# The norm between two layers: g and b applied on ScalarE where the output is transposed, and to the residual later

## The chip, the cores and the metric

The kernel runs on one core of a Trainium2 chip. The metric is the device time in microseconds (us) of one execution. A core has five engines that work side by side, each through its own list of instructions: TensorE (PE, matrix products; PEld is its loading of weights), VectorE (DVE), ScalarE (ACT), GpSimd (POOL) and SyncE (SP, which here only issues DMAs). Engines wait for one another through semaphores.

## The reference: what is computed

Two post-norm layers over 256 tokens of width 2048, in f32. A layer projects x, runs three groups of heads (chunked attention, gated linear attention, and cross-attention into 256 memory tokens), gates their outputs, projects back and normalizes:

```
h = x @ w_in                               # 6672 columns, split into the groups' inputs
mkv = mem @ w_mem_kv                       # memory keys and values
y = concat(y_a * silu(a_z), y_b * silu(b_z), y_m * silu(m_z))
out = y @ w_out
x = layer_norm(alpha * x + out, ln_g, ln_b)

layer_norm(x, g, b) = (x - mean(x)) * rsqrt(var(x) + 1e-5) * g + b      # over the 2048 columns
```

g and b are vectors over the 2048 columns, one pair for each layer. This case is about the norm that ends the first layer: its result is both the operand of the second layer's projections and the residual that the second layer adds at its own end.

## The kernel before, in words

*Weights and parts.* Every f32 weight is split into a high part and the low part that remains, and each product is made of three: high by high, low by high, high by low. A weight piece (`piece`, L129) is loaded by SP into `raw`, cast to its high part `wh` by ScalarE (L117) and subtracted to its low part `wl` by VectorE (L118); the pool `wp` holds four pieces of each kind. `parts` (L115) does the same for operands. These loads and splits are given a high priority (`AHEAD`).

*Two forms of projection.* In `ws_group` (L253) the weights are stationary and the result comes out transposed, in two halves of four pieces each; a piece is 16 matmuls. In `as_group` (L271) the tokens are stationary and the result has tokens on the partitions; it takes eight pieces (twelve matmuls each). Both call `tick()` after each piece.

*What sets the order.* PE and SP run their instructions as the program writes them (`manual_schedule`, L50). The order on VectorE, ScalarE and GpSimd is set at build time by a planner that weighs priorities against its own estimates of durations. The small work of the heads, and the transposition between layers, is written as generators: `tick()` (L53) takes the next due step of at most two active ones, and a step's `yield n` puts the next one n pieces later. `finish` (L70) runs ticks until the given generators are done, so steps that are left come back to back.

*The end of a layer.* The output projection runs over four column blocks of 512 (loop at L821, `as_group` at L862). After each block VectorE adds the residual (`add_residual`, L571) and takes statistics (L573). The residual `res` is one tile of 128 partitions, two token halves t, and 2048 columns. Rows of g and b for each block, spread over all 128 partitions, are loaded on POOL's queue into scratch buffers (L822 to L824); the eight of them are all of the pool `sc`.

*The norm between the layers* (`norm_between`, L575): the mean and variance (L581), `rstd` by `rsqrt` (L284: a square root on ScalarE, then four small VectorE instructions), and `nmr` = -mean * rstd (L583). Then eight chunks of res, a column block n by a token half t. Five are done by VectorE in two instructions each (L592, L593); three (`LN_POOL`, L30) by one ScalarE activation (L588) and a multiply and an add on GpSimd (L589, L590).

*The start of the second layer* (L734 to L743): the memory values G_MV by `as_group`, while the norm runs, then the memory keys G_MK by `ws_group`. Beside G_MK the generator `transposed` (L544) turns res into the operand of the projections: eight pairs of column blocks of 128, each with four PE transposes into a PSUM bank (L555), a cast to the high part by ScalarE and a subtract by VectorE (L556). It yields 2, so four pairs fit between the eight pieces of G_MK and the last four follow at once in `finish` (L743). The next projection, G_BQK (L748), uses this operand, a quarter (two pairs) to each piece; then come two value groups (L772, L773) and the gated linear attention (`gla`, L304), whose tiles `pairs0` and `pairs1` and whose output `yraw` (tags yr0 to yr3) matter below.

The last layer's norm (`norm_last`, L610) is a function of its own and is not touched.

Of the kernel before, what the change touches and what calls it, by code (L numbers as in the profile page):

```python
# [8 lines left out]
F32 = mybir.dt.float32  # L9
# [3 lines left out]
AF = mybir.ActivationFunctionType  # L13
ALU = mybir.AluOpType
# [4 lines left out]
P = 128  # L19
D = 2048  # L20
T = 256
# [5 lines left out]
RMS_EPS = 1e-6  # L27
LEVELS = (32, 16, 8, 4, 2, 1)
WO_N = 4
LN_POOL = ((1, 1), (2, 1), (3, 1))  # L30


G_MK, G_MV, G_BQK, G_AQ0, G_AK0, G_AQ1, G_AK1, G_MQ, G_BZ, G_AZ0, G_AZ1, G_MZ, G_WO = range(13)
# [4 lines left out]
def hybrid_trunk_kernel(  # L38
# [7 lines left out]
    pe, dve, act, pool, sp = nc.tensor, nc.vector, nc.scalar, nc.gpsimd, nc.sync  # L46
# [4 lines left out]
    waiting, active, done, now = [], [], set(), [0]  # L51

    def tick():  # L53

        now[0] += 1
        while True:
            while waiting and len(active) < 2:
                active.append((waiting.pop(0), 0))
            due = [e for e in active if e[1] <= now[0]]
            if not due:  # L60
                return
            active.remove(due[0])
            g = due[0][0]
            after = next(g, None)
            if after is not None:
                active.append((g, now[0] + after))
                return
            done.add(g)

    def finish(gens):  # L70
        while not all(g in done for g in gens):
            tick()

    def enter(name, bufs=1, **kw):
        return ctx.enter_context(tc.tile_pool(name=name, bufs=bufs, **kw))

    cst = enter("cst")
    per = enter("per")
    opp = enter("opp", 5)
    wp = enter("wp", 4)  # L80
    hd = enter("hd", 1)
# [7 lines left out]
    def nm(s):  # L89
        uid[0] += 1  # L90
        return f"{s}_{uid[0]}"
# [4 lines left out]
    def bank():  # L96
        return psa.tile([P, 512], F32, name=nm("bk"), tag="bk")

    def scratch(shape, dtype=F32):
        return sc.tile(shape, dtype, name=nm("sc"), tag="sc")  # L100

    def small(shape, tag, bufs=1):
        return sm.tile(shape, F32, name=nm(tag), tag=tag, bufs=bufs)

    ident = cst.tile([P, P], F32, name="ident")
# [4 lines left out]
    def operand():  # L110

        x = opp.tile([P, 4, 2, T], F32R, name=nm("x"), tag="x")
        return x[:, :, 0], x[:, :, 1], x.rearrange("p j h t -> p j (h t)")

    def parts(hi, lo, src):  # L115

        act.copy(hi, src)  # L117
        dve.tensor_tensor(lo, src, hi.bitcast(F32), op=ALU.subtract)  # L118
# [27 lines left out]
    def resident_quarter(q, src):  # L146

        with tc.high_priority(AHEAD):
            x = operand()
            sp.dma_start(early[:, q], src)  # L150
            parts(x[0], x[1], early[:, q])
        return x
# [388 lines left out]
        act.copy(y, po[:, :256])  # L541
        yield 2

    def transposed(xq):  # L544

        for q in range(4):
            x = operand()
            hi, lo, _ = x
            xq.append(x)
            for j in range(0, 4, 2):  # L550
                pt = bank()
                for jj in range(2):
                    kt = q * 4 + j + jj
                    for t in range(2):
                        pe.transpose(pt[:, jj * T + t * P:jj * T + (t + 1) * P], res[:, t, kt * P:(kt + 1) * P], ident)  # L555
                parts(hi[:, j:j + 2], lo[:, j:j + 2], pt.rearrange("p (j t) -> p j t", j=2))  # L556
                yield 2

    def columns(n):
        return slice(n * 512, (n + 1) * 512)  # L560
# [11 lines left out]
        for i in range(halves):  # L572
            dve.bn_stats(stats[:, t, 2 * n + i], r[:, i * 256:(i + 1) * 256])  # L573

    def norm_between(stats, gb):  # L575

        mvt = small([P, 2, 2], "mvt")
        rstd = small([P, 2], "rstd")
        nmr = small([P, 2], "nmr")
        for t in range(2):  # L580
            dve.bn_aggr(mvt[:, t], stats[:, t])  # L581
        rsqrt(rstd, mvt[:, :, 1], 2, 0)
        dve.scalar_tensor_tensor(nmr, mvt[:, :, 0], -1.0, rstd, op0=ALU.mult, op1=ALU.mult)  # L583
        for n in range(WO_N):
            for t in range(2):
                r = res[:, t, columns(n)]
                if (n, t) in LN_POOL:
                    act.activation(r, r, AF.Identity, bias=nmr[:, t:t + 1], scale=rstd[:, t:t + 1])  # L588
                    pool.tensor_tensor(r, r, gb[n][0], op=ALU.mult)  # L589
                    pool.tensor_tensor(r, r, gb[n][1], op=ALU.add)  # L590
                else:
                    dve.scalar_tensor_tensor(r, r, mvt[:, t, 0:1], gb[n][0], op0=ALU.subtract, op1=ALU.mult)  # L592
                    dve.scalar_tensor_tensor(r, r, rstd[:, t:t + 1], gb[n][1], op0=ALU.mult, op1=ALU.add)  # L593

    def norm_rows(l):

# [121 lines left out]
    res = per.tile([P, 2, D], F32, name="res")  # L718
# [5 lines left out]
    for l in range(L):  # L724
        mk = [per.tile([P, 4, T], F32R, name=nm("mk"), tag=f"mk{i}") for i in range(2)]
        mv = [per.tile([P, 2, 512], F32R, name=nm("mv"), tag=f"mv{i}") for i in range(2)]
        xq = []
        if l == 0:
            def each(p):
                if p in (2, 4, 6, 7):  # L730
                    xq.append(resident_quarter(len(xq), xT[len(xq)]))

            first_memory(mk, mv, each)
        else:  # L734
            memq = []
            parts(*mv, as_group(w512[l, G_MV], memq, 512, 2, memT))
            gens = [transposed(xq)]
            waiting.extend(gens)
            for i, a, b in ws_group(w512[l, G_MK], memq):
                tmp = scratch([P, 2, T])  # L740
                total(tmp, a, b)
                parts(mk[0][:, i:i + 2], mk[1][:, i:i + 2], tmp)
            finish(gens)  # L743

        yraw = [per.tile([P, 4, T], F32, name=nm("yr"), tag=f"yr{i}") for i in range(4)]
        gq = hd.tile([P, 2, T], F32, name=nm("gq"), tag="gq")
        gk = hd.tile([P, 2, T], F32, name=nm("gk"), tag="gk")
        for i, a, b in ws_group(w512[l, G_BQK], xq):  # L748
# [27 lines left out]
        bias = {}  # L776

        def load_bias(h):
            bias[h] = hd.tile([P, 384], F32, name=nm("bias"), tag="bias", bufs=4)
            sp.dma_start(bias[h], relw[l, h])  # L780

        load_bias(0)
        load_bias(1)
        gens = [[gla(*gp, gq, gk, asv, yraw[0])]]
        waiting.extend(gens[0])
        for half in range(2):
            values(2 + half)
            q = heads(G_AQ0 if half == 0 else G_AQ1)
            k = heads(G_AK0 if half == 0 else G_AK1)
# [12 lines left out]
        for i, g in enumerate((G_BZ, G_AZ0, G_AZ1, G_MZ)):  # L802
            y = operand()
# [13 lines left out]
        last = l == L - 1  # L817
        stats = small([P, 2, 2 * WO_N, 6], "stats")
        gb = []
        rows = norm_rows(l) if last else None  # L820
        for n in range(WO_N):  # L821
            g, b = scratch([P, 512]), scratch([P, 512])  # L822
            pool.dma_start(g, ln_g[l:l + 1, columns(n)].to_broadcast([P, 512]))
            pool.dma_start(b, ln_b[l:l + 1, columns(n)].to_broadcast([P, 512]))  # L824
            gb.append((g, b))
            src = wo_pieces(l, n)
            if last and n == WO_N - 1:


                accs = [psd.tile([P, 2, 512], F32, name=nm("acc"), tag="acc")[:, 0], bank()]  # L830
                rest = bank()[:, :256]
                ws = [piece(src[pc], 512) for pc in range(2)]

                spare = [operand()[2].rearrange("p (h k) n -> p h k n", h=2),
                         per.tile([P, 2, 2, 512], F32R, name=nm("late"), tag="asv")]
                homes = {pc: (x[:, 0], x[:, 1]) for pc, x in zip((2, 3), spare)}
                for pc in range(2, 8):
                    ws.append(piece(src[pc], 512, 2, homes.get(pc)))

                def products(t, k0, k1):  # L840
                    for kt in range(k0, k1):
                        as_products(accs[t], t, yq, ws[kt // 2], kt, kt % 2)

                for kt in range(4):
                    for t in range(2):
                        products(t, kt, kt + 1)
                products(0, 4, 16)

                def more(i):
                    if i == 0:  # L850
                        products(1, 4, 11)
                    elif i == 1:
                        products(1, 11, 12)
                        for kt in range(12, 16):
                            as_products(accs[1][:, :256], 1, yq, [w[:, :, :256] for w in ws[kt // 2]], kt, kt % 2)
                    else:
                        for kt in range(12, 16):
                            as_products(rest, 1, yq, [w[:, :, 256:] for w in ws[kt // 2]], kt, kt % 2, 12)

                norm_last(accs, rest, stats, gb, rows, more)  # L860
                break
            acc = as_group(src, yq, 512)  # L862
            for t in range(2):
                add_residual(n, t, acc[:, t], stats)
            if last:
                for t, i in ((0, 1), (1, 0), (1, 1), (1, 2)):
                    if i == n:
                        r = res[:, t, columns(n)]
                        dve.tensor_tensor(r, r, gb[n][0], op=ALU.mult)
        if not last:  # L870
            norm_between(stats, gb)


# [84 lines left out]
```

## Time and profile before

| | |
|---|---|
| median of 3 runs | 933.7 us (933.2 to 934.07) |
| the profiled execution | 935.35 us |
| its span, first to last instruction | 933.6 us |
| granted TensorE clock, mean | 0.995 |

A row of the timeline gives the start, the time in us, the engine, the line, the operation, out<-in with shapes, and how many were merged (xN); in brackets stands the idle time before it and what ended it. Grouped rows have the busy time in us, the mean of one in ns, and the idle time before with its releasers. A row of the waits has the total, the number of times and the longest. A row of the windows has the stretch, its length, the busy time and number of instructions of PE, PEld, DVE, ACT and POOL, then the granted clock, the share of the DMA engines and GB/s.

### The profile page before, as it was taken

Reading aid. Unit: us, or ns where it says so; the run is one execution under the profiler, and the core shown is the slowest. Engines: PE = TensorE matmul, PEld = TensorE weight load, DVE = VectorE, ACT = ScalarE, POOL = GpSimd, SP = SyncE. Lnnn points to the kernel's source line nnn. Section 1 sums busy time; section 2 is a strip of 40 time slices with the busy share of each in tenths; the row PEclk is TensorE's granted clock in tenths of the full one; section 3 lists DMA queues with packets and bytes.
Section 4 is the critical chain, followed back from the end, with each engine's and each line's share of the span. In section 5 each row is a group of like instructions: output and inputs, shape, how many; then the busy total and the mean of one; then the engine's idle time right before and its main releaser. Section 6 shows DMA issues by size and latency. Waiting matters only on the chain.

```text
span 933.6 us, 14256 instructions
## 1 busy us (share of the span) xinstructions
PE 924.3 (99%) x5532; PEld 813.4 (87%) x5532; DVE 585.0 (63%) x796; ACT 498.7 (53%) x716; POOL 29.6 (3%) x46
## 2 busy tenths in 40 slices
PE   9999999999999999999999999999999999999997
PEld 7889998998888888888878899889888888888885
DVE  6764487645565666555598545965556567566565
ACT  6644475375456655433465446645744576563440
POOL 1000000000000000000040000000000000010000
PEclk9999999999999999999999999999999999999998
DMA  8955855545544465755756465555555444676542
GB/s 300 336 185 178 303 198 163 175 150 195 184 158 158 158 199 190 254 191 185 235 175 230 141 202 184 198 167 174 186 173 171 161 163 154 202 235 215 192 148 90
DMA packets 64867, 178.75 MB, mean 191 GB/s; under 512 B 7032, under 2 KB 22936, under 8 KB 64544
## 3 DMA queue, kind: packets, MB, share of 16 engines
q1 hardware_dynamic: 62784, 173.04, 55.0%
q0 software_dynamic: 1728, 4.28, 1.9%
q8 instruction: 43, 0.70, 0.3%
q10 hardware_dynamic: 288, 0.52, 0.2%
q14 instruction: 24, 0.20, 0.1%
HBM read 175.69 MB, written 2.10 MB: 190 GB/s over the span
## 4 chain that ended last, share of the span: by engine, by line
PE 92%; DVE 3%; DMA 2%; issue 1%; ACT 1%; SPq 0%; DVEq 0%; ACTq 0%
PE acc L94 84%; PE bk L94 7%; DMA raw<-memT 1%; DVE wl L118 1%; DMA raw<-w 1%; PE bk L496 1%; DVE res L593 0%; PE bk L531 0%; ACT x L117 0%; DVE stats L573 0%; PE bk L555 0%; DVE res L627 0%; DVE res L571 0%; ACT wh L117 0%; DVE x L118 0%
## 5 line engine op out<-in xcount | busy, mean ns | idle before, releaser
L118 DVE TENSOR_TENSOR wl<-raw,wh 128x1024 fp32r<-128x1024 f32 (+3 forms) x323 | 375.1, 1164 | 257.3 <-ACT wh L117 252.9
L117 ACT CAST wh<-raw 128x1024 fp32r<-128x1024 f32 (+3 forms) x323 | 320.9, 995 | 337.3 <-PE acc L94 224.2
L94 PE MATMUL acc<-x,wh 128*128 128x512 f32 x1376 | 439.0, 400 | 0.0
L94 PE MATMUL acc<-wh,x 128*128 128x512 f32 (+1 forms) x1112 | 318.6, 368 | 0.1
L94 PEld LDWEIGHTS acc<-x,wl 128*128 128x128 f32 x1376 | 258.4, 188 | 62.9 <-DVE wl L118 2.1
L94 PE MATMUL acc<-x,wl 128*128 128x256 f32 x1376 | 271.3, 279 | 1.6 <-DVE wl L118 1.6
L94 PEld LDWEIGHTS acc<-wh,x 128*128 128x128 f32 x1112 | 205.0, 188 | 24.0 <-ACT wh L117 1.0
L94 PEld LDWEIGHTS acc<-x,wh 128*128 128x128 f32 x1376 | 211.8, 189 | 2.3 <-issue 0.3
L94 PE MATMUL acc<-wl,x 128*128 128x512 f32 (+1 forms) x556 | 204.3, 368 | 0.7 <-DVE wl L118 0.7
L94 PEld LDWEIGHTS acc<-wl,x 128*128 128x128 f32 x556 | 104.5, 188 | 13.6 <-DVE wl L118 1.8
L488 ACT ACTIVATE sc<-sc,mx 128x128 f32<-128x128 f32 (+1 forms) x32 | 14.4, 450 | 19.6 <-DVE mx L486 19.6
L481 DVE SCALAR_TENSOR_TENSOR sc<-bk,bias 128x384 f32<-128x384 f32 x16 | 8.9, 554 | 17.3 <-PE bk L94 17.3
L261 DVE SCALAR_TENSOR_TENSOR sc<-acc,sc 128x512 f32<-128x512 f32 x23 | 15.7, 682 | 0.0
L571 DVE SCALAR_TENSOR_TENSOR res<-res,acc 128x512 f32<-128x512 f32 x15 | 9.7, 683 | 9.3 <-PE acc L94 9.3
L812 DVE TENSOR_TENSOR sc<-sc,yr 128x512 f32<-128x512 f32 x16 | 11.0, 689 | 6.4 <-ACT sc L808 6.4
L260 ACT ACTIVATE sc<-acc 128x512 f32<-128x512 f32 x23 | 13.7, 594 | 0.0
L375 ACT ACTIVATE sc<-sc 128x512 f32<-128x512 f32 x12 | 7.6, 633 | 10.8 <-DVE sc L373 10.8
L94 PE MATMUL bk<-qk,qk 128*128 128x128 f32 (+1 forms) x64 | 13.1, 327 | 0.0
L94 PE MATMUL bk<-sc,asv 128*128 128x256 f32 (+1 forms) x64 | 13.0, 326 | 0.0
L118 DVE TENSOR_TENSOR x<-res,x 128x512 fp32r<-128x512 f32 (+2 forms) x14 | 10.4, 763 | 3.8 <-ACT x L117 3.8
L118 DVE TENSOR_TENSOR x<-raw,x 128x1024 fp32r<-128x1024 f32 x5 | 6.1, 1212 | 10.3 <-ACT x L117 10.3
L808 ACT ACTIVATE sc<-sc 128x512 f32<-128x512 f32 x16 | 10.1, 630 | 4.6 <-DVE sc L261 4.5
(192 smaller groups left out, 559.2 us busy)
## 6 DMA issues: line engine op xcount, KB each, us to landing
raw<-w SPq DMA_DIRECT2D x230, 512.0 KB, 3.9
raw<-w SPq DMA_DIRECT2D x64, 388.0 KB, 3.1
raw<-w SPq DMA_DIRECT2D x47, 256.0 KB, 3.3
bias<-relw SPq DMA_DIRECT2D x16, 192.0 KB, 3.7
res<-xT SPq DMA_DIRECT2D x4, 512.0 KB, 5.3
res<-xn SPq DMA_DIRECT2D x1, 2048.0 KB, 8.3
sc<-ln_g POOLq DMA_DIRECT2D x8, 256.0 KB, 5.0
sc<-ln_b POOLq DMA_DIRECT2D x8, 256.0 KB, 5.4
```

Source lines behind the costliest of these rows:

```text
L94: pe.matmul(o, l, r, start=start, stop=stop, skip_group_check=True)
L117: act.copy(hi, src)
L118: dve.tensor_tensor(lo, src, hi.bitcast(F32), op=ALU.subtract)
L260: act.mul(dst, b, scale)
L261: dve.scalar_tensor_tensor(dst, a, scale, dst, op0=ALU.mult, op1=ALU.add)
L375: act.activation(dd, dd, AF.Abs)
L481: dve.scalar_tensor_tensor(s, pb[:, :384], SCALE, bias[h], op0=ALU.mult, op1=ALU.add)
L488: act.activation(s[:, own[t]], s[:, own[t]], AF.Exp, bias=mx[:, t:t + 1], accum_out=zs[:, t:t + 1])
L496: pe.transpose(pt[:, i * P:(i + 1) * P], s[:, i * P:(i + 1) * P], ident)
L571: dve.scalar_tensor_tensor(r, r, ALPHA, acc, op0=ALU.mult, op1=ALU.add)
L808: act.activation(sz, sz, AF.Silu)
L812: dve.tensor_tensor(sz, sz, yraw[i][:, j:j + 2], op=ALU.mult)
```

## The change

In `norm_between`, ScalarE alone brings all eight chunks to (x - mean) * rstd, without g and b. g and b of the layer are also loaded as 32 rows of 128 (`norm_columns`, new) and transposed once by PE, so that each column block has its g and b as one number per partition in `gT`. In `transposed`, each block is copied from PSUM by ScalarE with that g as scale and that b as bias into a scratch tile y, one activation of 128x256 per block, two to a pair, and y is then split into parts. The residual still lacks g and b; a new generator, `restored`, multiplies and adds them on VectorE, one chunk to a step, while G_BQK and the first value groups run. For that the broadcast rows of g and b live on in the buffers of `yraw`, whose tiles for the second layer are taken later. GpSimd does no arithmetic in the norm.

```diff
-LN_POOL = ((1, 1), (2, 1), (3, 1))
...
-    def transposed(xq):
-
+    def transposed(xq, gbT):
+
+        raw, gT = gbT
+        pt = bank()
+        pe.transpose(pt[:, :32], raw[:32], ident[:32, :32])
+        dve.tensor_copy(gT, pt[:, :32])
         for q in range(4):
             x = operand()
             hi, lo, _ = x
             xq.append(x)
             for j in range(0, 4, 2):
                 pt = bank()
+                y = scratch([P, 2, T])
                 for jj in range(2):
                     kt = q * 4 + j + jj
                     for t in range(2):
                         pe.transpose(pt[:, jj * T + t * P:jj * T + (t + 1) * P], res[:, t, kt * P:(kt + 1) * P], ident)
-                parts(hi[:, j:j + 2], lo[:, j:j + 2], pt.rearrange("p (j t) -> p j t", j=2))
+                    act.activation(y[:, jj], pt[:, jj * T:(jj + 1) * T], AF.Identity, bias=gT[:, 16 + kt:17 + kt],
+                                   scale=gT[:, kt:kt + 1])
+                parts(hi[:, j:j + 2], lo[:, j:j + 2], y)
+                yield 2
+
+    def restored(gb):
+
+        for n in range(WO_N):
+            for t in range(2):
+                r = res[:, t, columns(n)]
+                dve.tensor_tensor(r, r, gb[n][0], op=ALU.mult)
+                dve.tensor_tensor(r, r, gb[n][1], op=ALU.add)
                 yield 2
...
-    def norm_between(stats, gb):
+    def norm_between(stats):
...
         for n in range(WO_N):
             for t in range(2):
                 r = res[:, t, columns(n)]
-                if (n, t) in LN_POOL:
-                    act.activation(r, r, AF.Identity, bias=nmr[:, t:t + 1], scale=rstd[:, t:t + 1])
-                    pool.tensor_tensor(r, r, gb[n][0], op=ALU.mult)
-                    pool.tensor_tensor(r, r, gb[n][1], op=ALU.add)
-                else:
-                    dve.scalar_tensor_tensor(r, r, mvt[:, t, 0:1], gb[n][0], op0=ALU.subtract, op1=ALU.mult)
-                    dve.scalar_tensor_tensor(r, r, rstd[:, t:t + 1], gb[n][1], op0=ALU.mult, op1=ALU.add)
+                act.activation(r, r, AF.Identity, bias=nmr[:, t:t + 1], scale=rstd[:, t:t + 1])
+
+    def norm_columns(l):
+
+        raw = hd.tile([P, P], F32, name=nm("gbrow"), tag="pairs0")
+        for i, src in enumerate((ln_g, ln_b)):
+            pool.dma_start(raw[i * 16:i * 16 + 16], src[l].rearrange("(k p) -> k p", p=P))
+        return raw, hd.tile([P, 32], F32, name=nm("gbT"), tag="pairs1")
...
-            gens = [transposed(xq)]
-            waiting.extend(gens)
+            gens = [transposed(xq, gbT), restored(gb)]
+            waiting.append(gens[0])
             for i, a, b in ws_group(w512[l, G_MK], memq):
...
-            finish(gens)
-
-        yraw = [per.tile([P, 4, T], F32, name=nm("yr"), tag=f"yr{i}") for i in range(4)]
+            finish(gens[:1])
+            waiting.append(gens[1])
+
...
         load_bias(0)
         load_bias(1)
+        if l > 0:
+            finish(gens)
+        yraw = [per.tile([P, 4, T], F32, name=nm("yr"), tag=f"yr{i}") for i in range(4)]
         gens = [[gla(*gp, gq, gk, asv, yraw[0])]]
...
-            g, b = scratch([P, 512]), scratch([P, 512])
+            if last:
+                g, b = scratch([P, 512]), scratch([P, 512])
+            else:
+                both = per.tile([P, 2, 512], F32, name=nm("gb"), tag=f"yr{n}")
+                g, b = both[:, 0], both[:, 1]
...
         if not last:
-            norm_between(stats, gb)
+            norm_between(stats)
+            gbT = norm_columns(l)
```

## The prediction

> **What bounds the kernel now.** First the page: span and busy shares.
>
> ```profile
> span 933.6 us, 14256 instructions
> PE 924.3 (99%) x5532; PEld 813.4 (87%) x5532; DVE 585.0 (63%) x796; ACT 498.7 (53%) x716; POOL 29.6 (3%) x46
> ```
>
> TensorE (PE) sets the end. Work taken from VectorE (DVE) or GpSimd (POOL) is worth only what it lets PE stop waiting. So the next view is PE's waits, cut to the stretch around the norm between the layers (455 to 511 us), and then PE's timeline for their places:
>
> ```profile
> PE acc L94 <- DVE wl L118: 2.1, 2, 1.6
> ```
>
> ```profile
> 475.01 0.50 PE L94 MATMUL acc<-wl,x 128*128 128x512 f32 x1 [0.41 <-DVE wl L118]
> ...
> 488.34 0.50 PE L94 MATMUL acc<-x,wl 128*128 128x256 f32 x2 [1.64 <-DVE wl L118]
> ```
>
> Two waits, 0.41 + 1.64 = 2.05 us, both for the low part (wl) of a weight piece. The ends of matmuls are modelled in this profile, so I measure the loss by starts as well. VectorE's residual add (L571) starts as soon as a column block of the output projection is summed:
>
> ```profile
> 395.30 1.28 DVE L571 SCALAR_TENSOR_TENSOR res<-res,acc 128x512 f32<-128x512 f32 x2 [0.63 <-PE acc L94]
> ...
> 438.82 1.28 DVE L571 SCALAR_TENSOR_TENSOR res<-res,acc 128x512 f32<-128x512 f32 x2 [0.64 <-PE acc L94]
> ```
>
> These are the first and the third block: two blocks of 96 matmuls take 43.52 us. After the third come the fourth block and the memory values of layer 1 (G_MV), 96 matmuls each, so the memory keys (G_MK) are due 43.52 after the third add, less the 0.20 by which a next block's first matmul leads the add (395.10 against 395.30):
>
> ```profile
> 395.10 0.61 PE L94 MATMUL acc<-wh,x 128*128 128x512 f32 x2
> ...
> 482.85 0.62 PE L94 MATMUL acc<-x,wh 128*128 128x512 f32 x2
> ...
> 485.63 0.60 PE L555 MATMUL bk<-ident,res 128*128 128x128 f32 x4
> ...
> 493.56 0.60 PE L555 MATMUL bk<-ident,res 128*128 128x128 f32 x4
> ...
> 505.62 0.60 PE L555 MATMUL bk<-ident,res 128*128 128x128 f32 x4
> ...
> 508.86 1.91 PE L555 MATMUL bk<-ident,res 128*128 128x128 f32 x16
> ```
>
> Due 438.82 + 43.52 - 0.20 = 482.14, in fact 482.85: **0.71 lost**. Inside G_MK a group of transposes stands after every second weight piece. From the first to the second group are 7.93 us; from the second to the fourth 12.06, so 6.03 each, for the same work: **1.90 lost**. Together 2.61 us is all that the norm costs PE and the ceiling of any gain here. One piece of G_MK takes 485.63 - 482.85 = 2.78.
>
> The Trainium skill, "Perfetto Trace Analysis", section "Per-engine timelines", says that a PE start is recorded while its end is only estimated; it would also choose the starts. By the idle column the ceiling would be 2.05 and the sum below 0.56 us worse.
>
> Who makes wl late? VectorE's timeline ahead of both waits, and ScalarE's (ACT) casts, which come piece by piece:
>
> ```profile
> 471.02 1.40 DVE L592 SCALAR_TENSOR_TENSOR res<-res,mvt,sc 128x512 f32<-128x512 f32 x2
> ...
> 473.73 1.22 DVE L118 TENSOR_TENSOR wl<-raw,wh 128x1024 fp32r<-128x1024 f32 x1
> ...
> 479.45 0.16 DVE L583 SCALAR_TENSOR_TENSOR nmr<-mvt,rstd 128x2 f32<-128x2 f32 x1
> 479.53 6.53 DVE L593 SCALAR_TENSOR_TENSOR res<-res,rstd,sc 128x512 f32<-128x512 f32 x5
> 485.99 6.77 DVE L118 TENSOR_TENSOR wl<-raw,wh 128x1024 fp32r<-128x1024 f32 x3
> ```
>
> ```profile
> 469.24 1.04 ACT L117 CAST wh<-raw 128x1024 fp32r<-128x1024 f32 x1
> ...
> 478.55 1.05 ACT L117 CAST wh<-raw 128x1024 fp32r<-128x1024 f32 x1 [1.82 <-DMA raw<-w]
> ...
> 481.78 1.03 ACT L117 CAST wh<-raw 128x1024 fp32r<-128x1024 f32 x1
> ...
> 485.64 1.05 ACT L117 CAST wh<-raw 128x1024 fp32r<-128x1024 f32 x1 [0.49 <-PE acc L94]
> ```
>
> The first late wl had its cast at 470.3, but VectorE did L592s first and began it at 473.73. The second had its cast at 479.6; five L593 held VectorE until 485.99. Beside GpSimd's part of the norm VectorE also ran slowly, as the groups show for 481 to 493 us, then for the whole run:
>
> ```profile
> L118 DVE TENSOR_TENSOR wl<-raw,wh 128x1024 fp32r<-128x1024 f32 x3 | 6.8, 2307 | 0.0
> L593 DVE SCALAR_TENSOR_TENSOR res<-res,rstd,sc 128x512 f32<-128x512 f32 x3 | 5.2, 1786 | 0.0
> ```
>
> ```profile
> L592 DVE SCALAR_TENSOR_TENSOR res<-res,mvt,sc 128x512 f32<-128x512 f32 x5 | 3.5, 743 | 0.0
> L118 DVE TENSOR_TENSOR wl<-raw,wh 128x1024 fp32r<-128x1024 f32 x250 | 307.6, 1234 | 181.1 <-ACT wh L117 180.6
> ```
>
> **The change part by part.**
>
> *Removed from VectorE:* five L592 (3.5) and five L593 (6.5), 10.0 us, and the slowing of three wl, 3 x (2.307 - 1.234) = 3.2. The first late wl can then start at 471.02, where the L592s began, and is done by 472.3; PE wants it at 475.01 - 0.71 = 474.3. The second can start at 479.6 and is done by 480.9; PE wants it at 486.4, or 485.7 with the first loss gone. Both waits go: **-2.61**. Next in line is the wl behind each, and those too would be some us early: 481.78 + 1.03 + 1.23 = 484.0 for one that PE wants 2.78 and more after 485.7.
>
> *Moved to ScalarE:* all eight chunks of the norm instead of three, then two more activations for each of eight pairs of transposed blocks.
>
> ```profile
> L588 ACT ACTIVATE res<-res,nmr,rstd 128x512 f32<-128x512 f32 x3 | 2.2, 807 | 0.0
> L469 ACT ACTIVATE yr<-bk,ng 128x256 f32<-128x256 f32 x8 | 3.1, 472 | 0.0
> L504 ACT COPY yr<-bk 128x256 f32<-128x256 f32 x16 | 5.8, 364 | 0.0
> L117 ACT CAST x<-sc 128x512 fp32r<-128x512 f32 x16 | 9.5, 617 | 1.0 <-DVE sc L812 1.0
> ```
>
> The chunks add 5 x 0.807 = 4.0 us. The new activation reads PSUM, 128x256, with a scale and a bias per partition. A plain copy of that shape takes 364 ns, one with one such operand 472. Bounds for two: 0.47 and 0.81 (L588, twice the columns). Another 108 ns gives an estimated 0.58, nearest to L469; I take that: 16 x 0.58 = 9.3 us. ScalarE gains some 13 us of work where it stands idle about half the time:
>
> ```profile
> 485.53:510.77 25.24, 23.60 (x148) 20.76 (x147) 20.99 (x19) 12.20 (x16) 6.72 (x5) 1.00 0.61 207
> 510.77:533.14 22.37, 22.37 (x130) 19.54 (x130) 12.30 (x15) 9.61 (x14) 0.00 (x0) 1.00 0.44 135
> ```
>
> After the length come PE, PEld, DVE, ACT, POOL: ScalarE is busy 12.20 of 25.24, then 9.61 of 22.37. Cost 0 while that idle time can be used; the rivals price it where the order forbids it. PE's first transposes, which will stand at 485.63 - 0.71 = 484.9, need only two chunks: even with nmr as late as now (479.6) they are done by 481.3.
>
> The Trainium skill, "ScalarE: Activation LUTs", section "Rules for kernel authors", speaks against this move: multiply and add belong on VectorE, up to about three times faster in bf16. This trace, in f32, has 807 ns for scale and bias together on ScalarE against two VectorE instructions of 743 each. At three times 743 the eight chunks would take an estimated 17.8 us, not 6.5, and rival C would be 12.3 by its sum.
>
> *Added on PE:* one small transpose of the 32 rows of g and b. Four full ones take 0.60 (above), so it costs 0 to **+0.15**; I take 0.15. It is ahead of the first group, and nothing else of PE's order moves.
>
> *Added on VectorE:* one 128x32 copy behind that transpose, between the 0.16 of 128x2 (L583) and the 0.68 of 128x512 below, which only the first pair waits for; and later 16 multiplies and adds on the residual:
>
> ```profile
> L869 DVE TENSOR_TENSOR res<-res,sc 128x512 f32<-128x512 f32 x4 | 2.7, 682 | 0.0
> ```
>
> They come two to every two pieces, from 511 us on: 8 x 0.68 = 5.5 us in the stretch to 533, where VectorE has 10.1 idle. One delays a wl by at most 0.7. The cast at 485.64 waited only for one of the four buffers that PE had just freed, so casts in step are three pieces (8 us) ahead: cost 0, up to 0.7 once if that lead is gone. GpSimd reads nothing beside them.
>
> *Moved or added on queues:* two small loads (the rows of g and b) on POOL's queue. GpSimd stood idle for 98 us before its first norm instruction:
>
> ```profile
> 480.55 3.26 POOL L589 TENSOR_TENSOR res<-res,sc 128x512 f32<-128x512 f32 x2 [98.00 <-ACT res L588]
> ```
>
> The loads wait for a buffer that the first layer's gated attention gave up long before, so they run in that gap; if they came late, PE would wait by just so much. The broadcast rows of layer 0 wait for the yr buffers in place of scratch and are wanted later than now. SP's order stays. Cost 0.
>
> Sum: -2.61 + 0.15 = -2.46, say **-2.5 us**. The profiled execution took 935.35 (span 933.6, 1.75 around it) and becomes 932.85; the median of the runs, 933.7, becomes **931.2**.
>
> **The rivals.**
>
> *B, the last four pairs come late.* Their 16 transposes end at 508.86 + 1.91 = 510.77; the next projection (G_BQK) then wants its third operand quarter two pieces later, the fourth at 519.1, and that one's second half at 520.5. ScalarE's queue there now:
>
> ```profile
> 508.87 1.05 ACT L117 CAST wh<-raw 128x1024 fp32r<-128x1024 f32 x1 [1.71 <-issue]
> 509.82 0.59 ACT L260 ACTIVATE sc<-acc 128x512 f32<-128x512 f32 x1
> 510.31 2.04 ACT L117 CAST x<-bk 128x512 fp32r<-128x512 f32 x4
> 512.21 0.66 ACT L117 CAST mk<-sc 128x512 fp32r<-128x512 f32 x1
> 513.41 1.05 ACT L117 CAST wh<-raw 128x1024 fp32r<-128x1024 f32 x1 [0.53 <-ACT mk L117]
> 516.19 1.05 ACT L117 CAST wh<-raw 128x1024 fp32r<-128x1024 f32 x1 [1.74 <-PE acc L94]
> ```
>
> A pair will cost 2 x 0.58 + 0.62 = 1.78, four of them 7.1. With all else ahead of the last pair: 508.87 + 1.05 + 0.59 + 7.1 + 0.66 + 2.1 = 520.4, and a 0.68 subtract, 521.05: 0.5 late, or 1.6 with one more cast in front. Against: the casts at 513.41 and 516.19 have the lead of 8 us and may stand behind. Price 0.9: **932.1**.
>
> *C, the block moves to ScalarE.* Eight chunks in a row from 479.65 (6.5) and the first pair (1.8) would hold the third key piece's cast, now at 481.78, until 487.9. Its wl is ready 1.05 + 1.23 later, 490.2. The piece begins at 482.14 + 2 x 2.78 + 0.60 + 0.15 = 488.45 and wants it 0.4 later: 1.3 lost, **932.5**. Against: without the L592s nmr should come sooner, and the casts have the higher priority.
>
> *D, slower: in ScalarE's order a pair's activations, which wait for PE's transposes, stand ahead of the cast of the very next piece.* PE then waits for pair, cast and subtract, 1.78 + 1.05 + 1.23 = 4.1 us a step. One step gives 935.3, still within the margin; it decides from the second on, **939.4**. Against: the cast at 485.64, beside the first pair, was for a piece three further on.
>
> **How the numbers follow.** A measurement of this kernel tells about 0.2% (1.9 us) from no change. Forecast 0.55 (0.50 faster, 0.05 within, since it lies only 0.6 beyond the margin); B 0.20 (0.02 faster, 0.18 within); C 0.10 (0.08 within, 0.02 slower); D 0.15, all slower. So faster 0.52, within 0.31, slower 0.17. The range goes from the whole ceiling and the half us of the runs' spread below, 930.6, to one step of D, 935.3; beyond lie D's two steps.
>
> **What would show it.** Right: no PE wait for wl between 455 and 511 us; transposes 6.0 apart throughout; wl at 1.23 everywhere; no PE wait for x after 508. B: a PE wait for x near 517 to 520. C: a PE wait for wl, with ScalarE full of chunks before it. D: ScalarE idle until PE's transposes with a cast behind. A new PE wait elsewhere, from another planned order of VectorE and ScalarE, would make the sum wrong at its root.

## The result, and the profile after

The changed kernel takes **948.23 us** (median of 4 runs, 947.05 to 948.47) against 933.88 for the kernel before (4 runs): ratio 1.0148, 95% interval 1.0135 to 1.016. It is slower by 14 us, where 2.5 us faster was forecast. The profiled execution took 947.05 with a span of 945.3, 11.7 more than before. It is the fastest of the four, so the sums below account for these 11.7 us; where the other executions spent the rest of the 14 is not shown.

First the head of the page of the changed kernel. Lines of this kernel's code after the change differ a little from before: matmuls are L93, casts L116, subtracts L117, the transposes of res L559, the new activations L560.

```profile
span 945.3 us, 14281 instructions
PE 927.4 (98%) x5533; PEld 814.8 (86%) x5533; DVE 583.1 (62%) x803; ACT 511.0 (54%) x737; POOL 19.6 (2%) x42
```

The engines' totals are much as foretold: ScalarE has 12.3 us more, GpSimd 10 less. None of that explains 11.7 us. Next PE's waits, cut to the stretch around the norm as the prediction cut them (here 455 to 525 us; the row is the same over the whole run):

```profile
PE bk L559 <- ACT sc L560: 10.3, 8, 2.1
```

The waits for wl that the prediction wanted to remove are gone from this stretch. In their place PE waits eight times, once in each pair of transposed blocks, and not for an operand: its *transposes* wait for ScalarE's new activation. PE's timeline shows where:

```profile
482.34 0.61 PE L93 MATMUL acc<-x,wh 128*128 128x512 f32 x2
...
485.38 0.44 PE L559 MATMUL bk<-ident,res 128*128 128x128 f32 x2
487.91 0.44 PE L559 MATMUL bk<-ident,res 128*128 128x128 f32 x2 [2.09 <-ACT sc L560]
...
493.77 0.38 PE L559 MATMUL bk<-ident,res 128*128 128x128 f32 x2
495.30 0.44 PE L559 MATMUL bk<-ident,res 128*128 128x128 f32 x2 [1.15 <-ACT sc L560]
...
501.17 0.38 PE L559 MATMUL bk<-ident,res 128*128 128x128 f32 x2
...
509.07 0.38 PE L559 MATMUL bk<-ident,res 128*128 128x128 f32 x2
...
513.67 0.38 PE L559 MATMUL bk<-ident,res 128*128 128x128 f32 x2
515.69 0.66 PE L559 MATMUL bk<-ident,res 128*128 128x128 f32 x4 [1.64 <-ACT sc L560]
517.24 0.92 PE L559 MATMUL bk<-ident,res 128*128 128x128 f32 x4 [0.89 <-ACT sc L560]
519.19 1.11 PE L559 MATMUL bk<-ident,res 128*128 128x128 f32 x4 [1.03 <-ACT sc L560]
520.99 0.69 PE L559 MATMUL bk<-ident,res 128*128 128x128 f32 x2 [0.69 <-ACT sc L560]
521.33 1.20 PE L93 MATMUL acc<-x,wh 128*128 128x512 f32 x2
```

Before, four transposes of a pair came as one row (x4). Now two come, a gap, then two more. The diff says why: the activation that reads block jj stands *inside* the loop over jj, between the transposes of the first and of the second block, and both blocks lie in the same PSUM bank `pt`. ScalarE's queue shows what the gap is made of:

```profile
486.25 1.04 ACT L116 CAST wh<-raw 128x1024 fp32r<-128x1024 f32 x1 [1.19 <-DMA raw<-w]
487.29 0.56 ACT L560 ACTIVATE sc<-bk,gbT 128x256 f32<-128x256 f32 x1
488.38 0.57 ACT L560 ACTIVATE sc<-bk,gbT 128x256 f32<-128x256 f32 x1 [0.53 <-PE bk L559]
...
493.74 1.05 ACT L116 CAST wh<-raw 128x1024 fp32r<-128x1024 f32 x1 [1.74 <-PE acc L93]
494.69 0.56 ACT L560 ACTIVATE sc<-bk,gbT 128x256 f32<-128x256 f32 x1
495.78 0.57 ACT L560 ACTIVATE sc<-bk,gbT 128x256 f32<-128x256 f32 x1 [0.53 <-PE bk L559]
```

PE ends a weight piece; that releases a cast for a later piece (1.05 us), which stands first in ScalarE's queue; only then comes the activation (0.56) that lets PE go on. The first pair also waits for the cast's load; without that it would have gained little, since its activation also needs `gT`, and VectorE's copy of it ended only at 487.2. So PE stands still for a cast that it does not need for long: the cast at 493.74 fills a buffer just given up, one of four, so by count it is for the fourth piece on, which PE begins about 12 us later, at 506.28. In the last four pairs, back to back, each pair pays anew.

There is a second loss behind the last four. The windows of 1 us, with the length, the busy time and count of PE, PEld, DVE, ACT and POOL, then the granted TensorE clock, the DMA share and GB/s:

```profile
516.00:517.00 1.00, 0.34 (x4) 0.10 (x1) 0.54 (x1) 0.83 (x2) 0.00 (x0) 1.00 0.05 16
517.00:518.00 1.00, 0.76 (x4) 0.52 (x4) 0.39 (x1) 1.00 (x3) 0.00 (x0) 0.74 0.89 201
518.00:519.00 1.00, 0.16 (x1) 0.00 (x0) 1.00 (x3) 1.00 (x3) 0.00 (x0) 0.50 0.76 307
...
523.00:524.00 1.00, 1.00 (x4) 0.81 (x4) 1.00 (x3) 0.00 (x0) 0.00 (x0) 0.50 0.00 0
524.00:525.00 1.00, 1.00 (x7) 0.92 (x6) 1.00 (x3) 0.00 (x0) 0.00 (x0) 0.84 0.00 0
525.00:526.00 1.00, 1.00 (x7) 0.85 (x6) 0.53 (x1) 0.47 (x1) 0.00 (x0) 1.00 0.00 0
```

From about 517.5 to 524.3 the clock (1.00, 0.74, 0.50 and so on, behind POOL's 0.00) is at half, and PE starts 4 matmuls in a microsecond, not 7.

**The sum by starts**, in the way of the prediction. The groups of transposes begin 8.39, 7.40 and 7.90 us apart against 6.03, and the fourth is followed by the last four pairs after 4.60 against 3.24 (the first experiment's trace, below): 2.36 + 1.37 + 1.87 + 1.36 = 7.0 us. The last four pairs take 513.67 to 521.33, 7.66, where 16 transposes in a row took 1.67 before: 6.0. The half clock costs the next projections 1.4: the gated attention's first copy (L334 on VectorE, at 581.5) comes 60.2 us after their start, not 58.8. The small transpose of g and b costs 0.26 (485.38 - 482.34 = 3.04 against 2.78). Less the 2.61 that did go: 7.0 + 6.0 + 1.4 + 0.3 - 2.6 = **12.0** (unrounded terms), and the trace gives 12.0 from the first residual add to that copy (186.0 against 174.1).

### The profile page after: what moved, and what is told of

It reads as the page before. It is cut to its first block, busy times and chain, and to the rows that moved or that the text cites. A ratio compares the mean times of both kernels' runs of the same rounds, so it can differ in the third digit from the quotient of the medians.

```text
span 945.3 us, 14281 instructions
## 1 busy us (share of the span) xinstructions
PE 927.4 (98%) x5533; PEld 814.8 (86%) x5533; DVE 583.1 (62%) x803; ACT 511.0 (54%) x737; POOL 19.6 (2%) x42
## 4 chain that ended last, share of the span: by engine, by line
PE 95%; ACT 2%; DVE 1%; DMA 1%; issue 0%; SPq 0%; ACTq 0%
PE acc L93 87%; PE bk L93 7%; DMA raw<-w 1%; ACT wh L116 1%; ACT sc L560 1%; PE bk L495 1%; PE bk L559 0%; PE bk L530 0%; DVE res L643 0%; PE bk L466 0%; DVE res L685 0%; DVE res L586 0%; DVE wl L117 0%; DVE stats L588 0%; ACT mk L116 0%
## 5 line engine op out<-in xcount | busy, mean ns | idle before, releaser
L117 DVE TENSOR_TENSOR wl<-raw,wh 128x1024 fp32r<-128x1024 f32 (+3 forms) x323 | 372.3, 1156 | 269.2 <-ACT wh L116 264.5
L116 ACT CAST wh<-raw 128x1024 fp32r<-128x1024 f32 (+3 forms) x323 | 321.0, 996 | 334.9 <-PE acc L93 231.5
L93 PE MATMUL acc<-x,wh 128*128 128x512 f32 x1376 | 440.2, 401 | 0.4 <-ACT wh L116 0.4
L93 PE MATMUL acc<-wh,x 128*128 128x512 f32 (+1 forms) x1112 | 318.6, 367 | 0.1
L93 PEld LDWEIGHTS acc<-x,wl 128*128 128x128 f32 x1376 | 259.0, 188 | 61.1
L93 PE MATMUL acc<-x,wl 128*128 128x256 f32 x1376 | 271.6, 279 | 0.0
L93 PEld LDWEIGHTS acc<-wh,x 128*128 128x128 f32 x1112 | 204.7, 188 | 24.1 <-ACT wh L116 1.1
L93 PEld LDWEIGHTS acc<-x,wh 128*128 128x128 f32 x1376 | 212.5, 190 | 3.0 <-ACT wh L116 0.8
L93 PE MATMUL acc<-wl,x 128*128 128x512 f32 (+1 forms) x556 | 203.9, 367 | 0.0
L93 PEld LDWEIGHTS acc<-wl,x 128*128 128x128 f32 x556 | 104.5, 188 | 12.5 <-DVE wl L117 0.7
L117 DVE TENSOR_TENSOR x<-sc,x 128x512 fp32r<-128x512 f32 x24 | 16.1, 686 | 3.4 <-ACT x L116 3.4
L559 PE MATMUL bk<-ident,res 128*128 128x128 f32 x32 | 7.1, 326 | 10.3 <-ACT sc L560 10.3
L116 ACT CAST x<-sc 128x512 fp32r<-128x512 f32 x24 | 14.5, 620 | 1.2 <-DVE sc L831 1.0
L559 PEld LDWEIGHTS bk<-ident,res 128*128 128x128 f32 x32 | 3.9, 156 | 12.6 <-ACT sc L560 12.5
L374 ACT ACTIVATE sc<-sc 128x512 f32<-128x512 f32 x12 | 7.6, 634 | 11.3 <-DVE sc L372 11.3
L117 DVE TENSOR_TENSOR x<-res,x 128x512 fp32r<-128x512 f32 (+2 forms) x14 | 10.4, 764 | 4.8 <-ACT x L116 4.6
```

Source lines behind the costliest of these rows:

```text
L93: pe.matmul(o, l, r, start=start, stop=stop, skip_group_check=True)
```

## The experiments

**Theory 1**: the second block's transposes wait until ScalarE has read the first block out of the same bank. **Theory 2** (rivals B and C of the prediction): ScalarE has too much to do. **Theory 3**: the later multiplies and adds on VectorE, or the moved buffers. Each is compared with the kernel before as timed beside it, which took 934.97 us for experiments 1 to 4 and 934.7, on another chip, for 5 to 8. "By starts" below is the stretch from the first residual add to the gated attention's first copy, 174.1 us in the kernel before.

### 1. The order alone undone

```diff
                     for t in range(2):
                         pe.transpose(...)
+                for jj in range(2):
+                    kt = q * 4 + j + jj
                     act.activation(y[:, jj], pt[:, jj * T:(jj + 1) * T], ...)
```

> The changed kernel with one thing moved: PE's four transposes of a pair come first, then ScalarE's two activations. Theory 1 (the second block's transposes wait until ScalarE has read the first block out of the same PSUM bank): all eight waits of PE on ScalarE (10.3 us) and the half clock go, and the forecast's sum is left, about 931.3 us. Theory 2 (ScalarE has too much to do, about 13 us more): the waits reappear as waits of the next projection on the operand x, above 940 us. Theory 3 (the 16 later VectorE instructions or the moved buffers cost the time): unchanged, 948.

Measured: 933.7 us, ratio 0.9991 (0.9982 to 1.0001). All eight waits are gone, and with them 14 us; theories 2 and 3 can't hold for those. But 2.5 us below before was forecast and about 1.3 came, with an interval that just reaches no change; by starts it is 1.4 (172.7). PE's timeline of this kernel:

```profile
485.61 0.66 PE L559 MATMUL bk<-ident,res 128*128 128x128 f32 x4
491.69 0.60 PE L559 MATMUL bk<-ident,res 128*128 128x128 f32 x4
497.72 0.60 PE L559 MATMUL bk<-ident,res 128*128 128x128 f32 x4
503.75 0.60 PE L559 MATMUL bk<-ident,res 128*128 128x128 f32 x4
506.99 1.91 PE L559 MATMUL bk<-ident,res 128*128 128x128 f32 x16
515.11 0.72 PE L93 MATMUL acc<-x,wh 128*128 128x512 f32 x2 [0.65 <-DVE x L117]
```

The groups are 6.0 apart throughout: the waits for wl are gone as reasoned. One wait for x is new, at the next projection, as rival B has it, though at its third operand quarter and not the fourth. VectorE's timeline tells what was ahead of that subtract:

```profile
512.57 1.88 DVE L573 TENSOR_TENSOR res<-res,gb 128x512 f32<-128x512 f32 x3
514.38 0.68 DVE L117 TENSOR_TENSOR x<-sc,x 128x512 fp32r<-128x512 f32 x1
```

Three of the adds that complete the residual, 1.88 us, stand in the planned order before a subtract that PE waits for. The prediction had the 16 multiplies and adds come from 511 us on, two to every two pieces; in this trace they begin at 492.2, and 15 of them are done before that subtract.

### 2. A bank for each block, the order as in the change

```diff
-                pt = bank()
                 y = scratch([P, 2, T])
                 for jj in range(2):
+                    pt = bank()
...
-                        pe.transpose(pt[:, jj * T + t * P:jj * T + (t + 1) * P], ...)
-                    act.activation(y[:, jj], pt[:, jj * T:(jj + 1) * T], ...)
+                        pe.transpose(pt[:, t * P:(t + 1) * P], ...)
+                    act.activation(y[:, jj], pt[:, :T], ...)
```

> The changed kernel, order untouched, but each block of 128 columns is transposed into a PSUM bank of its own (the pool has four). Theory 1 (same bank): PE no longer waits in the four pairs beside the memory keys; in the last four pairs, eight blocks go through four banks, so PE waits some 2 to 4 us there, once or twice. About 931.3 + 2 to 4, 933 to 936 us. If not the bank but the written order alone made PE wait: 948. Theory 2: above 940.

Measured: 935.02 us, ratio 0.9999 (0.999 to 1.0008), within the expected 933 to 936. PE's timeline at the last four pairs:

```profile
506.41 1.03 PE L559 MATMUL bk<-ident,res 128*128 128x128 f32 x8
508.43 1.81 PE L559 MATMUL bk<-ident,res 128*128 128x128 f32 x8 [0.99 <-ACT sc L560]
```

Four blocks (x8) go through the four banks, one wait for the first bank to come free, then the other four. In the pairs beside the memory keys there is no wait. So the written order harms because the two blocks share a bank. `bank()` hands out a whole bank as one tile of the program, so no run tells whether the wait goes by the bank or by the tile.

### 3. The interleaving put into the kernel before

```diff
                     for t in range(2):
                         pe.transpose(...)
-                parts(hi[:, j:j + 2], lo[:, j:j + 2], pt.rearrange("p (j t) -> p j t", j=2))
+                    act.copy(hi[:, j + jj], pt[:, jj * T:(jj + 1) * T])
+                dve.tensor_tensor(lo[:, j:j + 2], pt..., hi[:, j:j + 2].bitcast(F32), op=ALU.subtract)
```

> The kernel before with only the interleaving: ScalarE casts each block out of PSUM as soon as its two transposes are written, between the two blocks of a pair; the norm itself is as before, on VectorE, ScalarE and GpSimd. Theory 1: PE waits for ScalarE once in each of eight pairs, 1 to 2 us each, and the time is 942 to 948 us, though nothing of the norm has moved. Theories 2 and 3: 934, as before.

Measured: 948.0 us (943.5 to 951.55 in 4 runs), ratio 1.0138 (1.0112 to 1.0165). Its waits, in the execution at 951.55 us:

```profile
PE bk L555 <- ACT x L556: 10.1, 8, 3.6
```

Nothing of the norm has moved here, and the loss is close to that of the whole change: 13 us, eight waits, 10.1 us. The four runs lie 8 us apart, so its size is known only roughly.

### 4 and 5. The interleaving in the last four pairs alone, and in the first four alone

```diff
                     for t in range(2):
                         pe.transpose(...)
+                    if q >= 2:
+                        act.activation(y[:, jj], ...)
+                for jj in range(2) if not (q >= 2) else ():
+                    kt = q * 4 + j + jj
                     act.activation(y[:, jj], ...)
```

This is the first kernel; the second has q < 2 in both places.

> As the first experiment, but the last four pairs (those written back to back ahead of the next projection) keep the interleaved order. From the starts in the changed kernel's trace these four cost PE 6.2 us, and the lower granted clock after them 1.3: theory 1 gives 931.3 + 7.5 = 938.8 us, with the clock at half again from about 4 us after they begin. If the four pairs beside the memory keys carry the loss instead: 931.3.

> The other half of the fourth experiment: only the four pairs beside the memory keys keep the interleaved order, the last four have their four transposes first. From the starts in the changed kernel's trace these four cost PE about 7.0 us: theory 1 gives the first experiment's time plus 7, with the granted clock at 1 throughout, since PE has whole weight pieces between the waits. If the half clock comes with any wait of PE on ScalarE, it shows here too.

Measured: the last four alone 940.98 us, 7.3 above the first experiment (7.5 expected), ratio to before 1.0066 (1.0051 to 1.0081). The first four alone 942.56, ratio 1.0078 (1.0064 to 1.0092), some 9 above (7 expected). Both halves cost; neither carries the loss alone. In the fourth experiment the clock was at half from about 6 us after the last four pairs begin, 4 expected, for 6.8 us. The expectation on the clock was wrong for the first four. PE's timeline of that kernel, and its 1 us windows (length, PE busy and count, clock, DMA):

```profile
485.99 0.44 PE L559 MATMUL bk<-ident,res 128*128 128x128 f32 x2
488.59 0.69 PE L559 MATMUL bk<-ident,res 128*128 128x128 f32 x2 [2.16 <-ACT sc L561]
```

```profile
487.00:488.00 1.00, 0.00 (x0) 1.00 1.01 270
488.00:489.00 1.00, 0.41 (x3) 0.53 0.92 328
489.00:490.00 1.00, 1.00 (x5) 0.50 1.01 410
...
491.00:492.00 1.00, 1.00 (x5) 0.77 0.98 365
492.00:493.00 1.00, 1.00 (x8) 1.00 0.26 102
```

One gap of 2.2 us was enough here to halve the clock for 3.4 us. In the changed kernel the same first gap (2.09) left it at 1, while gaps of 1.6 and 0.9 close together came just before the half clock there. So the price of a gap does not follow from its length alone. By starts this kernel is 8.4 above the first experiment: the expected 7.0, and 1.4 more in the first group, where the clock fell; other small waits cancel.

### 6. The norm without GpSimd, nothing else of the change

```diff
-LN_POOL = ((1, 1), (2, 1), (3, 1))
+LN_POOL = ()
```

> The kernel before with all eight chunks of the norm on VectorE and none on GpSimd; the change's order and activations are not in it. If VectorE's block of norm instructions makes the two waits for wl (the prediction's reading), they stay about as long, since eight undisturbed second instructions of 0.74 us take 5.9 us against 6.5 now: within 0.7 us of before. If GpSimd's slowing of VectorE were the larger part, the second wait (1.9 us) would mostly go: 1.5 us or more faster.

Measured: 934.3 us, ratio 0.9993 (0.9984 to 1.0001): by time no difference that can be told, as the first reading expected. The trace says more:

```profile
478.45 0.50 PE L94 MATMUL acc<-wl,x 128*128 128x512 f32 x1 [0.81 <-DVE wl L118]
...
486.35 0.60 PE L555 MATMUL bk<-ident,res 128*128 128x128 f32 x4
492.39 0.60 PE L555 MATMUL bk<-ident,res 128*128 128x128 f32 x4
```

The second wait, 1.9 us before, is gone (groups 6.04 apart), though VectorE does more. But the waits ahead of it grew (0.29 and 0.81 us, where one of 0.41 was): by starts G_MK begins 1.7 us late, where it was 0.71, so 0.9 us is gained in all (173.2 against 174.1); the medians give 0.4. VectorE's timeline shows where the second wait went:

```profile
480.72 1.22 DVE L118 TENSOR_TENSOR wl<-raw,wh 128x1024 fp32r<-128x1024 f32 x1
...
482.12 5.38 DVE L593 SCALAR_TENSOR_TENSOR res<-res,rstd,sc 128x512 f32<-128x512 f32 x8
```

In the kernel before, the subtract that the second wait was for, the seventh since the last residual add, stood behind the block of L593. Here the block begins later and the seventh stands ahead of it. So the planned order changed together with GpSimd's part, and this experiment can't tell the two apart: GpSimd's share of the second wait stays open. It does show that VectorE's norm instructions make PE wait without GpSimd's, 1.7 us by starts.

### 7. The first experiment without the restoring of the residual

```diff
                 r = res[:, t, columns(n)]
-                dve.tensor_tensor(r, r, gb[n][0], op=ALU.mult)
-                dve.tensor_tensor(r, r, gb[n][1], op=ALU.add)
                 yield 2
```

> The first experiment without the 16 multiplies and adds that give the residual its g and b: that part of the computation is left out. In the first experiment's trace VectorE does three of them ahead of the first subtract of the last four pairs, and PE then waits 0.65 us for it. If they are the cause, that wait goes and the time is about 1 us below the first experiment's, some 2.3 us below before. If ScalarE's casts are late anyway (rival B as predicted), the wait stays and the time is that of the first experiment.

Measured: 932.89 us, ratio 0.998 (0.9971 to 0.9989), and no PE wait for x. It is 1.8 us below before, the first experiment 1.3, with intervals that overlap; by starts 172.2 against 172.7. But this kernel has a small wait of its own, of 0.16 us for wl, at 482.79 in the first piece of G_MK. By starts it costs 0.44: the first group of transposes begins 3.48 us after G_MK (485.49 - 482.01), 3.04 in the first experiment. Without it the 16 instructions, costed at nothing, come to 0.9 us. They cost by their place in VectorE's order, not by their sum: the subtract that began at 514.38 there begins at 512.54 here.

### 8. The first experiment with the pairs spread better

```diff
                 parts(hi[:, j:j + 2], lo[:, j:j + 2], y)
-                yield 2
+                yield 2 if q == 0 else 1
```

> The first experiment, and from the second quarter on a pair is written after every weight piece and not after every second, so that two pairs and not four are left for the end of the memory keys. All of the computation is in it. If the lump of four pairs costs the last 1 us, no PE wait for x is left: 2.3 to 2.6 us below before. If the earlier pairs collide with the casts of the weight pieces, PE waits for wl or wh instead: no better than the first experiment.

Measured: **932.82 us**, ratio 0.998 (0.9972 to 0.9989), with the whole computation in it. PE's timeline:

```profile
497.97 0.60 PE L559 MATMUL bk<-ident,res 128*128 128x128 f32 x4
501.21 0.60 PE L559 MATMUL bk<-ident,res 128*128 128x128 f32 x4
504.45 0.60 PE L559 MATMUL bk<-ident,res 128*128 128x128 f32 x4
507.69 1.47 PE L559 MATMUL bk<-ident,res 128*128 128x128 f32 x12
```

The lump at the end is 12 transposes and not 16 (one pair that was due there, two left over), and PE has no wait between 380 and 580 us. This version is faster than both kernels: 1.9 us below before, 15 below the change as made. From the first residual add to the gated attention's copy it needs 567.8 - 396.0 = 171.8 us against 569.4 - 395.3 = 174.1 before: 2.3 of the 2.46 of the prediction's sum.

## Why the prediction was wrong

*The bound and the ceiling* were right. PE sets the end, the two waits for wl were 2.61 us, and both went, in the changed kernel and in experiments 1, 7 and 8 (7 has a new one of 0.16). Experiment 8 gains 2.3 of the forecast 2.46.

**The step that failed** is "Moved to ScalarE", with its "Cost 0 while that idle time can be used; the rivals price it where the order forbids it". It counted ScalarE's new activations as work beside PE, 16 of an estimated 0.58 us; the trace has this row for them, least, median and greatest in ns:

```profile
L560 ACT ACTIVATE sc<-bk,gbT x16: 556/564/572, 487.3 to 521.7; 128x256 f32<-128x256 f32 x16
```

The size was right, and beside the point. The step asked only what waits *for* the activation's output, and not what waits for its *input* to be read. Eight times PE's next two transposes do, because the change writes them after the activation and into the same bank. Where a change adds a wait, the question is what is queued behind the waiting instruction: here that was all of PE. Experiment 3 shows the wait's cost with the norm left in place, experiment 1 the moved norm without the wait, experiment 2 that the shared bank is what makes it. The prediction did name "a new PE wait elsewhere" as what would make its sum wrong at the root, but looked for it in the planned order of VectorE and ScalarE; it came from the order written in the change.

The Trainium skill, "PSUM — Partial Sum Buffer", section "PSUM bank collisions raise a hardware error", says that two engines must not be in the same bank (and quadrant of partitions) at once, at whatever columns, and that accesses are to be guarded by bank and not by address. The traces agree as to the guard: two blocks at different columns of one bank wait (10.3 us), and in separate banks only the wait for a free one, 1.0 us, is left. No run here lets the engines meet in one bank, so what the chip would do is not shown.

*Added on PE:* the small transpose cost 0.26 us, above its bound of 0.15.

*Added on VectorE:* "cost 0" failed by 0.9 us by starts (experiments 1 and 7). The cover was there as a sum, but the planner ran the multiplies and adds some 19 us sooner than I had them, and put three adds ahead of a subtract that had no lead, while I had reasoned from the lead of the weight casts.

*The rivals.* B's wait for x came in the first experiment, but at another operand and by VectorE's order, not by ScalarE's load; that its price of 0.9 fits is luck. C did not come in the changed kernel, but came close. ScalarE's timeline there:

```profile
474.60 5.76 ACT L602 ACTIVATE res<-res,nmr,rstd 128x512 f32<-128x512 f32 x8
480.26 3.90 ACT L116 CAST wh<-raw 128x1024 fp32r<-128x1024 f32 x4
```

The eight chunks ran 5 us sooner than I had feared, but held four casts behind them. In the changed kernel PE just did not wait; in experiments 7 and 5 it waited 0.16 and 0.31 us for the wl of the first of these casts. (C's 12.3 for chunks of 17.8 us should read 12.6 by its own terms: 1.3 + 17.8 - 6.5. And the two VectorE instructions of 743 ns that were set against ScalarE's 807 also apply g and b, so that comparison is of unlike work.) D had the right side and, in ScalarE's order, the right kind of trouble (a cast and an activation ahead of PE), but at another place: I let PE wait for operands of later matmuls, not for a bank, and looked for evidence against it where casts led by three pieces. That lead doesn't help an instruction that waits for the bank now.

## What to carry to other kernels

When a consumer is moved into a loop that fills one PSUM bank in parts, look at the order of accesses to the *bank*: write all parts, then read, or give each part a bank. On the engine that sets the end, a wait for another engine costs that engine's whole queue ahead of it, here a cast of 1.05 us before an activation of 0.56. And idle time as a sum hides little on an engine whose order is planned: ask of each added instruction which waited-for one it may stand before.

## What the runs showed of the hardware

Gaps of PE halved its granted clock where I had expected none to: in experiment 5 after one gap of 2.2 us, for 3.4 us. In the changed kernel the clock stayed at 1 after the first gap of 2.1, but fell about 4 us after the last four pairs began, for 6.8 us, and in experiment 4 about 6 us after, also for 6.8. Experiment 3 has two spells at half, of 6.9 and 3.4 us. The Trainium skill, "TensorE: Matmul & The Clock Gate", section "Part 1: The HAM clock gate", gives one idle window of about 3.4 us, free-running, before the clock falls to half. The two levels agree with the rows here; the gaps that sufficed were shorter than that window, and the measured gaps decide.
